# A recurrent layer whose outputs are made with tokens on the partitions, and its two head norms taken along the free axis

## The chip, the cores and the metric

The kernel runs on one core of a Trainium2 chip. The time is device microseconds of one execution, and the number that counts is the median of the runs. A core has TensorE (PE, with its weight loads, PEld), VectorE (DVE), ScalarE (ACT), GpSimd (POOL) and queues that issue transfers (SP's above all). Each engine works off its own instructions in a fixed order; semaphores tie the engines together.

## The reference, cut to what matters

A trunk of two layers over 512 tokens of 1024 features. Layer 0 mixes tokens with a recurrence of 12 heads of 64 (in 6 pairs), beside attention to 256 memory tokens. Layer 1 is chunked attention. Each layer has an output projection and a gated feed-forward part. Here the head norms of the recurrence are what counts:

```python
kk = k_h * per_head(k_k)
kk = kk / jnp.maximum(jnp.sqrt(jnp.sum(kk * kk, axis=-1, keepdims=True)), 1e-12)
k_h = k_h * (1.0 + (a_h - 1.0) * per_head(k_a))
y = wkv7_scan(r_h, w_h, k_h, v_h, -kk, kk * a_h)
mean = jnp.mean(y, axis=-1, keepdims=True)
var = jnp.mean(jnp.square(y - mean), axis=-1, keepdims=True)
y = (y - mean) * lax.rsqrt(var + LN_X_EPS) * per_head(lnx_w) + per_head(lnx_b)
y = y + jnp.sum(r_h * k_h * r_k.astype(f32), axis=-1, keepdims=True) * v_h
out = y.reshape(bsz, seq, D_MIX).astype(h.dtype) * g
```

So there are two sums over the 64 features of each head and token: the key norm (kk) and the group norm (var; the values enter with their mean taken out, so the mean of y is zero).

## The kernel before, in words

Activations lie with features on the 128 partitions and the 512 tokens along the free axis; a tile of 128 features is a pair of heads. The recurrence is solved in 8 chunks of 64 tokens. Three generators work on a pair of heads:

- `prepare` (L566): projections of key, receptance and value (`dense`, L190 on: eight weight tiles in a high and a low part, hence the lines L198, L199 and L203), the decay, the key norm, the products within a chunk (L644), which go through DRAM (d1, Lr) to VectorE. There a forward substitution of 31 steps (L657 to L669, tiles Xs and Xu) runs, and its result goes back through DRAM (d2, Tt).
- `front` (L707): the products of keys and receptances in a chunk (L717, masked on VectorE at L720) and transposes to token rows (L731 to L745).
- `back` (L768): the remaining blocks of the inverse (L776 to L799), the chunk's matrices (L805 to L823), the outputs psy: the part within a chunk (L831) and, in a chain over chunks, the part from the state (L836 makes the next state, L837 adds it on VectorE, L841 adds the state's part to the outputs), then the group norm and the gate.

Both norms use `head_rsqrt` (L546): a tile of squares is the stationary side of four matmuls with a two-column selector (L550), which gives sums with tokens on the partitions, 128x8. VectorE takes the inverse root in ten small instructions (L222 to L226), copies it out to 128x512 (L556), and four transposes (L559) turn it back to features on the partitions. VectorE multiplies by it: L629 for the key norm, L857 for the group norm. After L857 come scale and bias on ScalarE (L858), the bonus on VectorE (L859), and `dst_mix` (L867): the gate (L868), and a transfer to DRAM for the first four pairs, or, for the last two, a split into a high part (L215) and a low part (L216), which the output projection reads.

`weave` (L82) sets the order in which the generators write their instructions: each `yield` states a cost and a wait in ns, and the generator that is furthest behind its share goes next. A scheduler then reorders within its own rules, so that the real order of each engine is seen only in the built program. A round of the loop at L909 runs `back` of pair n-1, `front` of pair n and `prepare` of pair n+1. After the loop, `back` of the last two pairs runs beside the memory attention and the first two tiles of the output projection (`out_ahead`, L317 on), which are started without the last pair's features; `out_proj` adds these, with the residual add at L334, and takes the remaining six tiles. The residual x is loaded (L955) once the recurrent layer's buffers are free.

## Time and profile before

| what | value |
|---|---|
| median of 3 runs | 1376.41 us (1375.87 to 1377.62) |
| profiled execution | span 1375.2 us; the record holds no other time of this execution |
| TensorE's mean granted clock | 0.989 of full speed |
| busy: PE, PEld, VectorE, ScalarE, GpSimd | 1320.1, 1073.8, 827.1, 612.6, 34.0 us |
| chain that ended last | PE 78%, DVE 12%, ACT 4%, DMA 3%, issue 2% |
| transfers | 139.18 MB, mean 101 GB/s |

The span runs from the first to the last instruction. An engine is busy while an instruction of it is in flight; matmuls overlap one another, so a group of matmuls is priced by the distance from its start to the start of what follows it, not by the sum of its durations. Idle time of an engine is given with what ended it. Nearly all of the time after some 385 us is feed-forward and attention, which the change doesn't touch; the recurrent layer lies between some 50 and 372 us.

### The profile page before, as it was taken

To read this page: it belongs to the slowest core of one execution; us is meant where nothing else is said; L and a number is where in the kernel's file an instruction comes from. 1 tells how busy PE (TensorE), PEld (TensorE's weight loads), DVE (VectorE), ACT (ScalarE), POOL (GpSimd) and SP (SyncE) were. 2 spreads that over 40 slices of the span, in tenths; PEclk is the share of its full clock that TensorE was granted. 3 is DMA by queue.
4 is the path that set the end of the run, shared out by engine and by line. 5 is a ranking of instruction groups with operands and counts; after the bars stand their busy time and mean duration, and the time that the engine had idled before them with its cause. 6 is when DMAs were issued, how large, how long until landed. Compare 5 with 4: busy or idle time off the path is not lost.

```text
span 1375.2 us, 20877 instructions
## 1 busy us (share of the span) xinstructions
PE 1320.1 (96%) x8266; PEld 1073.8 (78%) x8266; DVE 827.1 (60%) x1752; ACT 612.6 (45%) x1022; POOL 34.0 (2%) x55
## 2 busy tenths in 40 slices
PE   6989999999799999999999999999999999999996
PEld 4877777777588888888888878786788888888886
DVE  7876788878356655655333667657665565563324
ACT  6556565555234333333222566657443333332321
POOL 3000000000000000000000000000000000000000
PEclk9999999999899999999999999999999999999998
DMA  5366544462132233233232422222223223223332
GB/s 181 112 181 135 107 104 111 104 135 50 52 117 92 92 100 100 92 97 99 84 98 85 157 87 85 82 94 94 92 92 107 92 93 103 96 88 86 106 91 75
DMA packets 63507, 139.18 MB, mean 101 GB/s; under 512 B 24625, under 2 KB 28337, under 8 KB 63409
## 3 DMA queue, kind: packets, MB, share of 16 engines
q1 hardware_dynamic: 60672, 127.89, 29.8%
q0 software_dynamic: 2736, 9.96, 4.2%
q8 instruction: 65, 1.06, 0.3%
q14 instruction: 34, 0.27, 0.1%
HBM read 131.01 MB, written 6.82 MB: 100 GB/s over the span
## 4 chain that ended last, share of the span: by engine, by line
PE 78%; DVE 12%; ACT 4%; DMA 3%; issue 2%; SPq 0%; DVEq 0%; ACTq 0%; POOLq 0%
PE psf L198 12%; PE psf L199 12%; PE psf L203 12%; PE psd L198 10%; PE psd L199 10%; PE psd L203 10%; DVE Xu L667 2%; DVE Xs L669 1%; PE pss L1098 1%; DVE Xs L662 1%; DVE ML L720 1%; DVE wlo L175 1%; PE psd L1048 1%; PE pss L297 1%; ACT whi L169 1%
## 5 line engine op out<-in xcount | busy, mean ns | idle before, releaser
L175 DVE TENSOR_TENSOR wlo<-wraw,whi 128x1024 fp32r<-128x1024 f32 x183 | 219.0, 1197 | 132.3 <-PE psd L203 118.2
L169 ACT CAST whi<-wraw 128x1024 fp32r<-128x1024 f32 (+1 forms) x202 | 207.8, 1030 | 163.9 <-DMA wraw<-in_ffn_out_dram 41.5
L198 PE MATMUL psd<-r1h,whi 128*128 128x512 f32 x336 | 137.6, 410 | 7.5 <-ACT r1h L215 3.8
L198 PE MATMUL psf<-r2h,whi 128*128 128x512 f32 x352 | 137.1, 390 | 0.0
L198 PE MATMUL psf<-r1h,whi 128*128 128x512 f32 x352 | 137.1, 390 | 0.0
L199 PE MATMUL psf<-r1l,whi 128*128 128x512 f32 x352 | 136.9, 389 | 0.0
L199 PE MATMUL psf<-r2l,whi 128*128 128x512 f32 x352 | 136.9, 389 | 0.0
L199 PE MATMUL psd<-r1l,whi 128*128 128x512 f32 x336 | 134.9, 401 | 0.2 <-DVE r1l L216 0.2
L203 PE MATMUL psd<-r1h,wlo 128*128 128x512 f32 x336 | 91.3, 403 | 3.9 <-DMA wlo<-in_wA_dram 3.9
L199 PE MATMUL psd<-f3l,whi 128*128 128x512 f32 (+1 forms) x238 | 88.6, 377 | 0.0
L198 PE MATMUL psd<-f3h,whi 128*128 128x512 f32 (+1 forms) x238 | 88.5, 376 | 0.0
L359 DVE TENSOR_TENSOR tmp<-psf,rho 128x512 f32<-128x512 f32 x44 | 30.4, 692 | 94.7 <-PE psf L203 94.7
L203 PE MATMUL psf<-r1h,wlo 128*128 128x512 f32 x352 | 86.9, 389 | 0.0
L203 PE MATMUL psf<-r2h,wlo 128*128 128x512 f32 x352 | 86.9, 389 | 0.0
L198 PEld LDWEIGHTS psd<-r1h,whi 128*128 128x128 f32 x336 | 65.0, 193 | 23.7 <-ACT r1h L215 4.0
L198 PE MATMUL psd<-r2h,whi 128*128 128x512 f32 (+1 forms) x200 | 77.0, 389 | 0.8 <-ACT r2h L1105 0.7
L199 PE MATMUL psd<-r2l,whi 128*128 128x512 f32 (+1 forms) x200 | 76.4, 385 | 0.7 <-DVE r2l L216 0.7
L198 PEld LDWEIGHTS psf<-r2h,whi 128*128 128x128 f32 x352 | 66.1, 188 | 13.7
L199 PEld LDWEIGHTS psf<-r1l,whi 128*128 128x128 f32 x352 | 66.1, 188 | 13.7
L203 PEld LDWEIGHTS psf<-r1h,wlo 128*128 128x128 f32 x352 | 66.1, 188 | 13.7
L203 PEld LDWEIGHTS psf<-r2h,wlo 128*128 128x128 f32 x352 | 66.1, 188 | 13.7
L199 PEld LDWEIGHTS psf<-r2l,whi 128*128 128x128 f32 x352 | 66.1, 188 | 13.6
(352 smaller groups left out, 2420.9 us busy)
## 6 DMA issues: line engine op xcount, KB each, us to landing
wraw<-in_ffn_in_dram SPq DMA_DIRECT2D x88, 512.0 KB, 3.3
wraw<-in_ffn_out_dram SPq DMA_DIRECT2D x32, 448.0 KB, 3.3
wraw<-in_wA_dram SPq DMA_DIRECT2D x20, 512.0 KB, 3.9
wlo<-in_wA_dram POOLq DMA_DIRECT2D x17, 512.0 KB, 8.0
wraw<-in_w_out_dram SPq DMA_DIRECT2D x16, 512.0 KB, 3.4
wraw<-in_ffn_out_dram SPq DMA_DIRECT2D x16, 512.0 KB, 4.2
wraw<-in_wB_dram SPq DMA_DIRECT2D x8, 512.0 KB, 3.4
Lr<-d SPq DMA_DIRECT2D x24, 128.0 KB, 6.3
```

The costliest lines, as they stand in the source:

```text
L169: SC.copy(hi[:, :n], raw)
L175: V.tensor_tensor(lo[:, :n], raw, hi[:, :n], op=ALU.subtract)
L198: PE.matmul(ps, wh[:, j * P:(j + 1) * P], ah, start=start and n == 0, stop=False)
L199: PE.matmul(ps, wh[:, j * P:(j + 1) * P], al, start=False, stop=False)
L203: PE.matmul(ps, wl[:, j * P:(j + 1) * P], act(k)[0], start=False, stop=stop and n == len(ks) - 1)
L297: PE.matmul(pso[hs, :], vm[l][:, kt, (f * 2 + hh) * 64:(f * 2 + hh + 1) * 64], pts[f, hh, kt], start=kt == 0, stop=kt == 1)
L359: V.tensor_tensor(v[:], pv[:], rho[:], op=ALU.mult)
L662: V.scalar_tensor_tensor(X[:, m, q + 1:], L1[:, :, 0], X[:, m, q:q + 1], X[:, m, q + 1:], op0=ALU.mult, op1=ALU.add)
L667: V.tensor_tensor(uv, L1.rearrange("p i o -> p o i").to_broadcast([P, k, n]), X[:, 0:k, q:q + 1].to_broadcast([P, k, n]), op=ALU.mult)
L669: V.tensor_tensor(X[:, 0:k, q + 1:], X[:, 0:k, q + 1:], uv, op=ALU.add)
L720: V.tensor_tensor(ML[:, h, c4 * 4:c4 * 4 + 4, 0:128], ps[h][:], C("m1").unsqueeze(1).to_broadcast([P, 4, 128]), op=ALU.mult)
L1048: PE.matmul(pt, r1h[:, k, ts], wh[:, ws], start=k == 0, stop=False)
```

## The change

The outputs psy are made the other way round: the operands of L831 and L841 swap sides, so that psy holds tokens of a chunk on the partitions and features along the free axis. The group norm then needs no matmul: VectorE sums the squares along the free axis, takes the inverse root and multiplies. After that, sixteen 64x64 matmuls with the identity turn the result back to features on the partitions, and ScalarE applies scale and bias on its way out of PSUM. In the key norm the squares are turned by four transposes and summed by VectorE from PSUM, in place of the four matmuls with the selector; the way back stays. Some stated costs and waits for `weave` change with it.

```diff
-    def head_rsqrt(sq, sel, fix, bank):
+    def head_rsqrt(sq, bank):
         ps = bank()
         for t in range(4):
-            PE.matmul(ps[:, 2 * t:2 * t + 2], sq[:, t * P:(t + 1) * P], C(sel), start=True, stop=True)
+            PE.transpose(ps[:, t * P:(t + 1) * P], sq[:, t * P:(t + 1) * P], C("ident"))
         a = kt_("hra", (P, 8), bufs=2)
-        fix(a[:], ps[:, 0:8])
+        V.tensor_reduce(a[:], ps[:].rearrange("p (g c) -> p g c", c=64), axis=AX.X, op=ALU.add)
+        V.tensor_scalar(a[:], a[:], 1e-24, None, op0=ALU.max)
         r = rsqrt_small(kp, a[:], 8)
-        yield 700, 3000
+        yield 600, 3500
...
-                PE.matmul(psy[HS[h], c], VT[:, h, c], ML[:, h, c, 64:128], start=c == 0, stop=False)
+                PE.matmul(psy[HS[h], c], ML[:, h, c, 64:128], VT[:, h, c], start=c == 0, stop=False)
...
-                    PE.matmul(psy[HS[h], c], St[HS[h], c], MQ[HS[h], c, 0:64], start=False, stop=c == 7)
+                    PE.matmul(psy[HS[h], c], MQ[HS[h], c, 0:64], St[HS[h], c], start=False, stop=c == 7)
...
         sq = tmp()
         SC.activation(sq[:], yc[:], AF.Square)
-        yield 0, 1700
-        hr = head_rsqrt(sq, "hsm", lambda o, p: V.tensor_scalar(o, p, LN_X_EPS, None, op0=ALU.add), ps_s)
-        yield next(hr)
-        pr_ = next(hr)
+        a = kt_("hra", (P, 8), bufs=2)
+        V.tensor_reduce(a[:], c3(sq[:]), axis=AX.X, op=ALU.add)
+        V.tensor_scalar(a[:], a[:], 1.0 / 64, LN_X_EPS, op0=ALU.mult, op1=ALU.add)
+        r = rsqrt_small(kp, a[:], 8)
+        V.tensor_tensor(c3(yc[:]), c3(yc[:]), r[:].unsqueeze(2).to_broadcast([P, NCH, 64]), op=ALU.mult)
+        yield 0, 5000
         if go is not None:
             yield go
+        pt = ups()
+        for c, h, ap, vp in U:
+            PE.matmul(pt[ap, c], yc[ap, c * 64:c * 64 + 64], cst[ap, I64:I64 + 64], start=True, stop=True)
         pg = ps_l()
         mm3(pg[:], g2h[:], g2l[:], gsh[:], gsl[:], True, True)
-        V.tensor_tensor(yc[:], yc[:], pr_[:], op=ALU.mult)
-        SC.activation(yc[:], yc[:], AF.Identity, scale=Vc("lnx_w", i), bias=Vc("lnx_b", i))
+        yc = tmp()
+        SC.activation(yc[:], pt[:].rearrange("p c t -> p (c t)"), AF.Identity, scale=Vc("lnx_w", i), bias=Vc("lnx_b", i))
         V.tensor_tensor(yc[:], yc[:], bon[:], op=ALU.add)
         dst(i, yc, pg)
-        yield 1080
+        yield 1680
```

The lines below the first edit move down by one, those behind the group norm by six. Three places show how the built order changes. First VectorE, at the key norm of the pair that the third steady round prepares. Xu and Xs are the substitution's tiles, hra the sums, rsq the inverse root. Before:

```order
L667 TENSOR_TENSOR Xu<-Lr,Xs 128x75
L626 TENSOR_SCALAR hra<-pss 128x8
L669 TENSOR_TENSOR Xs<-Xs,Xu 128x5x15
L222 TENSOR_SCALAR rsq<-hra 128x8
L667 TENSOR_TENSOR Xu<-Lr,Xs 128x70
```

And with the change:

```order
L670 TENSOR_TENSOR Xs<-Xs,Xu 128x5x15
L552 TENSOR_REDUCE hra<-pss 128x8
L668 TENSOR_TENSOR Xu<-Lr,Xs 128x70
L553 TENSOR_SCALAR hra<-hra 128x8
L670 TENSOR_TENSOR Xs<-Xs,Xu 128x5x14
L222 TENSOR_SCALAR rsq<-hra 128x8
```

The reduction over 128x512 stands where a small instruction stood, one more small instruction follows it, and the inverse root begins about one substitution step later.

Second VectorE again, at the end of the group norm in the same stretch (bon is the bonus, psl the gate, ML the masked products). Before:

```order
L556 COPY tmp<-rsq 128x512
L857 TENSOR_TENSOR tmp<-tmp,pss 128x512
L859 TENSOR_TENSOR tmp<-tmp,bon 128x512
L720 TENSOR_TENSOR ML<-pss,cst 128x4x128
L868 TENSOR_TENSOR tmp<-tmp,psl 128x512
L720 TENSOR_TENSOR ML<-pss,cst 128x4x128
```

And with the change:

```order
L226 SCALAR_TENSOR_TENSOR rsq<-rsq_2603,rsq 128x8
L854 TENSOR_TENSOR tmp<-tmp,rsq 128x512
L865 TENSOR_TENSOR tmp<-tmp,bon 128x512
L874 TENSOR_TENSOR tmp<-tmp,psl 128x512
L721 TENSOR_TENSOR ML<-pss,cst 128x4x128 x2
```

The copy is gone, the multiply stands ahead of the matmuls that turn the result, and between it and the bonus only PE and ScalarE lie.

Third PE, at the last pair's group norm, among the first two tiles of the output projection (psd). Before, from the second tile's sixth weight tile on:

```order
L199 MATMUL psd<-r1l,whi 128x512
L550 MATMUL pss<-cst,tmp 128x2 x4
L198 MATMUL psd<-r1h,whi 128x512
...
L203 MATMUL psd<-r1h,wlo 128x512 x7
L559 MATMUL pss<-cst,tmp 128x128 x4
L198 MATMUL psd<-r1h,whi 128x512
L199 MATMUL psd<-r1l,whi 128x512
```

And with the change:

```order
L199 MATMUL psd<-r1l,whi 128x512
L860 MATMUL pss<-cst,tmp 64x64 x16
L198 MATMUL psd<-r1h,whi 128x512
...
L203 MATMUL psd<-r1h,wlo 128x512 x7
L198 MATMUL psd<-r1h,whi 128x512 x2
L199 MATMUL psd<-r1l,whi 128x512
```

The sixteen matmuls stand where the sums stood, with the same eight and seven matmuls behind them, and nothing stands where the turned scale stood; the next L198 is the one that needs the last pair.

## Rows read from the trace of the kernel before

**Rows 1.** The page's first part: busy us, share of the span, instructions.

```profile
PE 1320.1 (96%) x8266; PEld 1073.8 (78%) x8266; DVE 827.1 (60%) x1752; ACT 612.6 (45%) x1022; POOL 34.0 (2%) x55
```

**Rows 2.** Busy time by stretch: stretch, length, engines (instructions), PE clock, DMA share, GB/s.

```profile
178.00:220.00 42.00, 40.04 (x509) 31.25 (x509) 34.16 (x121) 23.48 (x43) 3.45 (x4) 1.00 0.56 121
329.00:347.00 18.00, 17.90 (x271) 13.22 (x269) 12.98 (x42) 11.96 (x33) 0.00 (x0) 1.00 0.11 35
375.00:380.00 5.00, 3.14 (x7) 2.48 (x8) 4.24 (x6) 2.38 (x4) 0.00 (x0) 0.50 0.97 344
```

**Rows 3.** PE in order of time, a steady round: start, length, instruction [idle before].

```profile
193.90 1.15 PE L644 MATMUL pss<-KB,AR 64*64 64x64 f32 x32
194.85 0.31 PE L841 MATMUL psl<-MQ,W 64*64 64x64 f32 x4
...
205.71 0.95 PE L550 MATMUL pss<-cst,tmp 128*128 128x2 f32 x8
206.52 0.48 PE L198 MATMUL psd<-r1h,whi 128*128 128x512 f32 x1
...
210.51 0.60 PE L559 MATMUL pss<-cst,tmp 128*128 128x128 f32 x4
211.04 0.69 PE L781 MATMUL pss<-Tl,ML 32*32 32x32 f32 x32
...
231.52 0.63 PE L559 MATMUL pss<-cst,tmp 128*128 128x128 f32 x4 [0.81 <-DVE Xu L667]
```

**Rows 4.** VectorE in order of time: first round (107.80) and steady rounds.

```profile
107.80 0.17 DVE L626 TENSOR_SCALAR hra<-pss 128x8 f32<-128x8 f32 x1 [1.77 <-PE pss L550]
...
189.22 0.23 DVE L667 TENSOR_TENSOR Xu<-Lr,Xs 128x48 f32<-128x48 f32 x1
...
209.36 0.17 DVE L226 SCALAR_TENSOR_TENSOR rsq<-rsq,rsq 128x8 f32<-128x8 f32 x1
209.56 0.43 DVE L556 COPY tmp<-rsq 128x512 f32<-128x512 f32 x1
...
213.40 0.69 DVE L859 TENSOR_TENSOR tmp<-tmp,bon 128x512 f32<-128x512 f32 x1 [1.56 <-ACT tmp L858]
214.00 0.68 DVE L720 TENSOR_TENSOR ML<-pss,cst 128x512 f32<-128x512 f32 x1
...
230.95 0.42 DVE L556 COPY tmp<-rsq 128x512 f32<-128x512 f32 x1
```

**Rows 5.** PE in order of time, the end of the recurrent layer.

```profile
362.48 0.95 PE L550 MATMUL pss<-cst,tmp 128*128 128x2 f32 x8
...
366.84 0.60 PE L559 MATMUL pss<-cst,tmp 128*128 128x128 f32 x4
371.23 0.50 PE L198 MATMUL psd<-r1h,whi 128*128 128x512 f32 x1 [3.79 <-ACT r1h L215]
...
376.86 0.80 PE L198 MATMUL psd<-r1h,whi 128*128 128x512 f32 x1 [2.57 <-DVE xT L334]
...
381.72 0.63 PE L199 MATMUL psd<-r1l,whi 128*128 128x512 f32 x1
382.15 0.52 PE L198 MATMUL psd<-r1h,whi 128*128 128x512 f32 x1
```

**Rows 6.** ScalarE in order of time, the same stretch.

```profile
355.38 0.63 ACT L848 ACTIVATE tmp<-tmp 128x512 f32<-128x512 f32 x1
368.26 0.81 ACT L858 ACTIVATE tmp<-tmp,vec 128x512 f32<-128x512 f32 x1 [12.26 <-DVE tmp L857]
...
372.62 1.04 ACT L169 CAST whi<-wraw 128x1024 fp32r<-128x1024 f32 x1 [1.45 <-PE psd L199]
```

**Rows 7.** VectorE in order of time, the same stretch.

```profile
371.21 0.69 DVE L216 TENSOR_TENSOR r1l<-tmp,r1h 128x512 fp32r<-128x512 f32 x1 [0.69 <-ACT r1h L215]
```

**Rows 8.** The reduction of the memory attention (L270): ns min/median/max, first and last start.

```profile
L270 DVE TENSOR_REDUCE mst<-pss x16: 670/684/692, 320.3 to 867.4; 128x2 f32<-128x512 f32 x16
```

**Rows 9.** SP's queue in order of time, the same stretch: the loads of x.

```profile
371.96 1.75 SPq L955 DMA_DIRECT2D xT<-in_xT_dram  x4
```

More of the change, by code (lines that the diff above doesn't have):

```diff
@@ L625, in keys @@
             SC.activation(sq[:], kn[:], AF.Square)
-            hr = head_rsqrt(sq, "hs1", lambda o, p: V.tensor_scalar(o, p, 1e-24, None, op0=ALU.max), ps_s)
+            hr = head_rsqrt(sq, ps_s)
             yield next(hr)
@@ L848, in back @@
         SC.activation(sq[:], yc[:], AF.Square)
-        yield 0, 1700
-        hr = head_rsqrt(sq, "hsm", lambda o, p: V.tensor_scalar(o, p, LN_X_EPS, None, op0=ALU.add), ps_s)
-        yield next(hr)
-        pr_ = next(hr)
+        a = kt_("hra", (P, 8), bufs=2)
[4 more added lines that the diff above has]
+        yield 0, 5000
         if go is not None:
             yield go
+        pt = ups()
+        for c, h, ap, vp in U:
+            PE.matmul(pt[ap, c], yc[ap, c * 64:c * 64 + 64], cst[ap, I64:I64 + 64], start=True, stop=True)
         pg = ps_l()
         mm3(pg[:], g2h[:], g2l[:], gsh[:], gsl[:], True, True)
-        V.tensor_tensor(yc[:], yc[:], pr_[:], op=ALU.mult)
-        SC.activation(yc[:], yc[:], AF.Identity, scale=Vc("lnx_w", i), bias=Vc("lnx_b", i))
+        yc = tmp()
+        SC.activation(yc[:], pt[:].rearrange("p c t -> p (c t)"), AF.Identity, scale=Vc("lnx_w", i), bias=Vc("lnx_b", i))
         V.tensor_tensor(yc[:], yc[:], bon[:], op=ALU.add)
         dst(i, yc, pg)
-        yield 1080
-    BACK_COST = 2 * 650 + 2 * MC + 4 * 1100 + 1700 + 6 * 150 + 7 * 150 + 700 + 1080
+        yield 1680
+    BACK_COST = 2 * 650 + 2 * MC + 4 * 1100 + 1700 + 6 * 150 + 7 * 150 + 1680
     mixd = dp.tile([4, P, S], F32, name="mixd", tag="mixd")
```

## The prediction

> **What bounds the kernel now.** I read the busy line first: PE has matmuls in flight for 96% of the span [rows 1], so a gain must take work from PE or close a gap in front of it. The recurrent layer holds nearly all that the change touches, so I then read busy times by stretch. Its steady part is a round of some 42 us, four of them from 136 to 304 us; in one, PE is busy for 40 us of 42 and VectorE for 34 [rows 2]. The gaps are small, and the question is which engine ends each part of a round.
>
> PE in order of time answers that [rows 3]. A round has two fixed points: the matmuls that turn the group norm's scale (L559, 210.51 us) and those that turn the key norm's scale (L559 again, 231.52 us). Ahead of the first PE did not wait. So the half of the round that ends there, half B, is set by PE. Ahead of the second PE idled 0.81 us for VectorE. So half A, between the two, is set by VectorE, which from the bias add at 213.40 to the copy that ends at 231.37 runs without a gap worth naming [rows 4]: it works off the 31 steps of the forward substitution, and the key norm's small instructions stand between them.
>
> Then the end of the recurrent layer. The last pair's group norm has nothing recurrent behind it. Its sums stand on PE at 362.48, behind output-projection matmuls, and its turned scale at 366.84; PE then waits 3.79 us for the finished pair and 2.57 us more for a bank [rows 5]. This is the longest hole in the layer, and the chain through it is: multiply, ScalarE's scale and bias, bias add, gate, cast, split [rows 6, 7].
>
> **The change part by part.**
>
> *Key norm (six times).* Four matmuls with a two-column moving side become four transposes. The first take 0.81 us until the next matmul starts (205.71 to 206.52), the second 0.53 (210.51 to 211.04) [rows 3]: PE saves 0.28 us. VectorE adds a sum over 128x512. Such a reduction costs 684 ns here [rows 8]; queued behind other work it takes about 0.60 of the engine, the distance of a 0.69 us instruction from its successor (213.40 to 214.00) [rows 4]. The clamp stays at 0.16. In half A this addition is on the path, since VectorE ends that half.
>
> The Trainium skill speaks against it ("VectorE: DVE Perf Modes", Rules for kernel authors): a reduction on a hot path is called the slowest operation of the engine, better restructured away. By the row it is as slow as a bias add of the same shape (0.69) and no slower. By the page the outcome would be the first rival, 1381.1; by the row it is the sum below.
>
> *Group norm (six times).* On PE the sums (0.81) and the turned scale (0.53) go; sixteen 64x64 matmuls come. The nearest row is the sixteen of L644, 193.90 to 194.85, 0.95 us [rows 3]: 0.39 saved. On VectorE a copy (0.42) and a multiply (0.69, as the bias add of the same shape) become a reduction and a multiply: +0.26. The path to the bias add shortens. Before, 2.89 us lie between L559's start and the bias add (210.51 to 213.40), of them 1.56 of waiting [rows 3, 4]. After, the turned result goes straight through ScalarE: 0.95 on PE, 0.81 on ScalarE [rows 6] and two hand-overs, 2.0 us. VectorE starts its long run 0.9 us earlier against PE.
>
> *Outputs with swapped operands.* Both sides have 64 columns before and after, in the same number of passes: 0. Bounds: one weight load of a state less or more per chunk, hidden under output projections or weights in the rounds; I keep +-0.2.
>
> *A round, half A.* -0.9 for the earlier bias add, +0.60 for the reduction. In two of three rounds the new order also puts one more pair of substitution steps ahead of the copy, 0.23 us each, 0.5 with the gaps [rows 4]. Sum +0.2, and -0.3 without that pair. PE's saving there is not seen: PE would only wait longer.
>
> *Half B.* The sums' 0.81 leave PE. In the new order about 0.5 us more of the projection stands in this half, taken from half A where PE waits anyway. The new chain (copy and square on ScalarE, 0.6 each; reduction and multiply, 0.69 each; eleven small instructions 0.20 apart [rows 4, 6]) takes 4.8 us and some 0.5 of hand-overs after the last output matmul. The order holds 22 to 24 wide matmuls over it, 5.2 to 5.7 us at the 0.24 that they take at the end of the layer, so it is covered; where that cover is thin, a gap of up to 0.5 us opens. Sum -0.3, with -0.8 if nothing moved. A round: about -0.2; four rounds -0.9. Bounds: -0.7 a round if PE's saving counted in full (-2.8), +1.0 a round if the reduction, the pair of steps and a wait for the key product all count against only the earlier bias add (+4.0).
>
> *First round and first pair.* Here VectorE waited 1.77 us for the key norm's sums [rows 4], so the reduction lies bare in the chain: +0.6, less 0.28 on PE; with the wait behind it I take +0.5 (0 to +0.8).
>
> *The pair before last.* It runs beside memory attention, where PE is busy 17.9 of 18 us [rows 2]: PE's saving counts, -0.4 (0 to -0.5).
>
> *The last pair.* In the new order the sixteen matmuls take the place of L550, and nothing takes the place of L559. Their input is ready by about 359.8: the square ends at 356.0 [rows 6], then reduction, eleven small ones and multiply, 3.6 us. So no wait at 362.48. They end at 363.43. The fifteen projection matmuls behind them took 3.55 us (0.81 after 362.48, to 366.84; 0.24 each), so PE is at the waiting matmul at 366.98. From ScalarE's scale and bias (368.26) to PE's restart (371.23) it was 2.97 us; now that chain starts at 363.5, so the operand is there at 366.5 and the wait of 3.79 goes [rows 5, 6]. The split of the low half ended at 371.90 and will end at 367.15, and the loads of x that are issued on its end (371.96) go out 4.75 earlier [rows 7, 9]. What is late next: the weights of the third output tile. ScalarE's cast waits for PE to release a buffer (372.62); a second cast, two subtractions and the residual add follow on it, and PE gets its bank at 376.86 [rows 5, 6]. These links keep their lengths, from 367.4 on: bank at 371.95. Gain 4.9 us. PE will then idle longer there, 3.6 us instead of 2.57.
>
> The clock is the unknown. After the 3.79 us gap the granted clock fell to 0.50 from 375 to 380 us, its lower level of 1.2 GHz [rows 2], and matmuls stayed 0.43 us apart (381.72 to 382.15) until then [rows 5]. Between 376.86 and 382.15 this costs 5.3/2 = 2.65 us. I assume the same length of slow running behind the remaining gap. Bounds: none (2.65 more gained), or as long as from the first restart, 10.9 us (2.8 us given back): -2.1 to -7.5.
>
> **The sum.** -0.9 + 0.5 - 0.4 - 4.9 = -5.7 us on the profiled execution's span of 1375.2; that gives 1369.5. The median of the runs, 1376.41, is 1.2 above this span, so I forecast 1370.7.
>
> **The rivals.**
>
> *VectorE becomes the bound (slower).* Place: the key norm in the five rounds that hold a substitution. If reduction (0.60), pair of steps (0.5) and a wait of about 1 us for the key product behind it all add up, and half B ends on VectorE too, a round gets 2.0 us longer: +10, less 5.3 at the end, +4.7: 1381.1. For it: VectorE's unbroken run in half A. Against: the bias add comes earlier, and VectorE has some 8 us of idle time per round. It decides from a round that is 1.1 us longer than now. 8 in 100. This is what the caution of the Trainium skill above ("VectorE: DVE Perf Modes", Rules for kernel authors) comes to in this kernel; the trace bears it out in half A only.
>
> *The end gives little.* If the gap that is left keeps the clock low for as long as before, the end brings 2.1, and the rounds come out even: 1376.4 - 2.1 + 0.5 = 1374.8. For it: the remaining gap is nearly as long as the one that went. 21 in 100.
>
> *PE's saving counts everywhere.* Five rounds at -0.7, the end 4.9, the pair before last 0.4: -8.8, 1367.6. Against it speaks the wait in half A. 11 in 100.
>
> *Forecast* as above, 60 in 100, its own range 1367 to 1374.
>
> **Numbers.** The range 1366.0 to 1377.0 takes in the end at both bounds and the rounds from -2.8 to about +3. A measurement here can tell about 0.2%, 2.75 us, so faster means below 1373.7. There lie 0.56 of the forecast's 0.60 and all of the third rival: 0.67. Same: the second rival and 0.03 of the forecast, 0.24. Slower, above 1379.2: the first rival and the last 0.01, 0.09.
>
> **What would show it.** The wait of 3.79 us before the first output tile gone, the wait for the bank (2.57) grown by about a microsecond, and the loads of x issued some 4.8 us earlier against the last output matmul. In the rounds: waits of PE at the key norm's turn grown from 0.8 towards 1.5 us, waits of VectorE for L550 and L559 gone from the group norm, rounds of 41.5 to 42.5 us. I am wrong if rounds exceed 43 us, if PE waits at the new sixteen matmuls, or if the low clock after the end outlasts some 8 us.

## The result, and the profile after

The changed kernel takes 1384.77 us (median of 13 runs, 1379.51 to 1392.24) against 1376.89 (13 runs, 1374.77 to 1382.22) for the kernel before: ratio 1.0051, with a 95% interval of [1.0035, 1.0067]. It is **slower by 7 us**, half a percent: little, but clear of the noise. The forecast was 1370.7 with a range to 1377.0, so sign and size were both missed.

The page's first part of the changed kernel, and its line by core:

```profile
PE 1328.6 (96%) x8362; PEld 1077.7 (78%) x8362; DVE 834.2 (60%) x1758; ACT 614.5 (44%) x1022; POOL 33.7 (2%) x55
```

```profile
core 0: 1390.5 us, clock 0.977
```

PE has 96 more instructions and is busy 8.5 us longer [rows 1]. By the counts in the rows the group norm now issues 32 of them for a pair where it issued 12, and the key norm four fewer, for six pairs. They are short ones; what changed is the speed. Span times mean granted clock, an estimate of what the span would be at full clock, is 1375.2 x 0.989 = 1360.1 before and 1390.5 x 0.977 = 1358.5 after. Taken from each run's device time and clock, the median of this product is 1361.8 for the changed kernel (13 runs) and 1360.8 for the kernel before (the 29 runs of experiment 2). **By this estimate the two kernels would take the same time at full clock, to about 1 us; the difference in time is the size of the clock that TensorE lost.** That is a balance: the changed kernel does less work at the end and waits more before it, and the waits are what the low clock follows.

This execution was the slowest of the 13; a second profile comes from another one (1385.73 us, span 1384.0, clock 0.984). By fixed points of PE:

| stretch, end in the kernel before | forecast | first profile | second profile |
|---|---|---|---|
| start to the third pair's key turn (146.66) | +0.5 | +3.4 | +4.0 |
| to the group turn of the fourth round (295.28) | -0.9 | +9.1 | +6.2 |
| to the last pair's turn or sums (362.48) | -0.4 | +7.1 | +4.0 |
| to the end | -4.9 | -4.3 | -5.4 |
| sum | -5.7 | +15.3 | +8.8 |

I call *lost clock* the sum of (1 - granted clock) x 5 us over slices of 5 us from 0 to 400 us. It is 10.2 us before, 27.2 in the first and 18.8 in the second profile: in the second the 8.6 us more are nearly the whole 8.8 us of the span. By stretch it is not all clock: in the rounds (second line of the table) some 5 of the 9.1 us and 3.4 of the 6.2 are lost clock, and the rest is mostly the new waits themselves.

**The end went as forecast.** PE in order of time, changed kernel (start, length, instruction, idle before):

```profile
373.86 0.48 PE L842 MATMUL psd<-AR,Lr 64*64 64x64 f32 x4 [0.27 <-DVE AR L838]
...
382.04 1.15 PE L860 MATMUL pss<-cst,tmp 64*64 64x64 f32 x32
...
391.64 0.79 PE L198 MATMUL psd<-r1h,whi 128*128 128x512 f32 x1 [3.43 <-DVE xT L334]
```

and SP's queue:

```profile
386.92 1.78 SPq L961 DMA_DIRECT2D xT<-in_xT_dram  x4
```

The wait of 3.79 us is gone, and the bank wait grew from 2.57 to 3.43 [rows 5]. From the last output matmul to the loads of x it is 13.1 us (386.92 - 373.86) where it was 17.6 (371.96 [rows 9] - 354.38): 4.5 earlier, 4.8 forecast.

**The rounds did not.** In two profiles of this kernel three rounds from key turn to key turn took 42.6, 47.4, 45.2 and 42.9, 42.8, 46.3 us, where before they took 42.1 to 42.8. PE now waits at the sixteen matmuls (L860). PE, then VectorE, in the second round:

```profile
192.62 0.63 PE L560 MATMUL pss<-cst,tmp 128*128 128x128 f32 x4 [1.47 <-DVE Xu L668]
...
216.42 1.63 PE L860 MATMUL pss<-cst,tmp 64*64 64x64 f32 x32 [2.01 <-DVE tmp L854]
```

```profile
210.51 0.69 DVE L851 TENSOR_REDUCE hra<-tmp 128x8 f32<-128x512 f32 x1 [0.24 <-ACT tmp L849]
212.59 0.43 DVE L777 STREAM_TRANSPOSE Tl<-Tt 32x256 f32<-32x256 f32 x1 [1.39 <-DMA Tt<-d]
212.96 0.12 DVE L852 TENSOR_SCALAR hra<-hra 128x8 f32<-128x8 f32 x1
...
215.59 0.69 DVE L854 TENSOR_TENSOR tmp<-tmp,rsq 128x512 f32<-128x512 f32 x1
```

VectorE works in order. Between the reduction (L851) and the small instruction behind it (L852) stands L777, the transpose of the solved blocks, and it waits 1.39 us for their load from DRAM (Tt). All of the norm's root and the multiply (L854) stand behind, and PE behind them. The place is not new. In the kernel before, both transposes (L776 there) stood among the root's small instructions as well:

```profile
206.78 0.42 DVE L776 STREAM_TRANSPOSE Tl<-Tt 32x256 f32<-32x256 f32 x1
207.69 0.43 DVE L776 STREAM_TRANSPOSE Tl<-Tt 32x256 f32<-32x256 f32 x1
```

They waited in none of the four rounds; what is new is that the load is late for them. Busy time by stretch, changed kernel, columns as in [rows 2]:

```profile
212.00:217.00 5.00, 2.99 (x29) 2.29 (x28) 3.28 (x14) 2.11 (x2) 0.86 (x1) 0.99 0.42 89
217.00:222.00 5.00, 5.00 (x70) 4.41 (x68) 2.29 (x4) 1.51 (x3) 0.00 (x0) 0.50 0.82 167
```

Behind the wait of 2.01 us the clock is at its lower level (0.50, 1.2 GHz): the wait costs 2 us, the slow matmuls behind it 2.5 more from 217 to 222 us. Not every such wait is followed by that. In the second profile PE waits as long in the fourth round, and the clock stays full:

```profile
305.43 1.15 PE L860 MATMUL pss<-cst,tmp 64*64 64x64 f32 x32 [2.00 <-DVE tmp L854]
```

```profile
305.00:310.00 5.00, 4.57 (x122) 4.31 (x124) 3.42 (x7) 2.09 (x4) 0.45 (x1) 1.00 0.66 129
```

Why the load is late shows in the queues, third round, SP and GpSimd, changed kernel:

```profile
253.51 0.36 SPq L180 DMA_DIRECT2D wraw<-in_wA_dram  x1
254.08 3.08 SPq L676 DMA_DIRECT2D Tt<-d  x4
```

```profile
253.78 0.86 POOL L173 DMA_DIRECT2D wlo<-in_wA_dram  x1 [9.03 <-ACT wlo L172]
```

The weights of the next pair (wraw, 512 KB, and the accumulating load of their low half, wlo, 512 KB) go out ahead of the solved blocks, and L777 waited for these until 263.04, 2.21 us. Before, the blocks went out at 244.76 and wlo only at 245.81. In the second round it is wlo alone: 206.34 against 206.97 for the blocks, where before the blocks went out at 202.18 and wlo at 203.68. In the fourth the blocks still go out first, at 298.61, but wlo follows at 298.92 where it came 0.98 us behind them, and L777 waits 1.66 us. Where the wait falls differs too: in the second and fourth rounds it stands inside the norm's chain (L860 waits 2.01 and 1.74 us); in the third the wait of 2.21 us stands behind the multiply, L860 waits 0.54 us, and the matmuls that take the blocks (L782) wait 1.24.

**Memory attention lost as much.** PE beside the memory attention, changed kernel:

```profile
334.95 0.33 PE L837 MATMUL psl<-W,MQ 64*64 64x64 f32 x4 [1.62 <-DVE W L838]
...
336.26 0.44 PE L837 MATMUL psl<-W,MQ 64*64 64x64 f32 x4 [0.46 <-DVE W L838]
```

```profile
330.00:335.00 5.00, 3.38 (x23) 2.34 (x21) 5.00 (x11) 1.89 (x6) 0.00 (x0) 1.00 0.17 26
335.00:350.00 15.00, 14.27 (x74) 8.57 (x75) 9.44 (x30) 8.02 (x26) 0.00 (x0) 0.54 0.19 49
```

PE waits 1.62 us for the second state update of the pair before last, and then runs 15 us at a mean clock of 0.54, 6.9 us lost. Before, PE waited 0.38 us there and ran memory attention at 1.00 [rows 2]. VectorE was busy for all of 330 to 335 with work that stands ahead of the update:

```profile
331.58 1.28 DVE L216 TENSOR_TENSOR r1l<-tmp,r1h 128x512 fp32r<-128x512 f32 x2
332.78 0.69 DVE L270 TENSOR_REDUCE mst<-pss 128x2 f32<-128x512 f32 x1
333.38 1.22 DVE L175 TENSOR_TENSOR wlo<-wraw,whi 128x1024 fp32r<-128x1024 f32 x1
...
334.63 0.27 DVE L838 SCALAR_TENSOR_TENSOR W<-psl,dE,VT 128x64 f32<-128x64 f32 x1
```

The subtractions L216 stood ahead of this update in the kernel before too, from 316.82 us; L175 (1.22 us) did not, there it starts at 327.38, behind the fifth update.

### The profile page after: what moved, and what is told of

It is laid out like the page before. It is cut to its first block, busy times and chain, and to the rows that moved or that the text cites. A ratio compares the mean times of both kernels' runs of the same rounds, so it can differ in the third digit from the quotient of the medians.

```text
span 1390.5 us, 21086 instructions
## 1 busy us (share of the span) xinstructions
PE 1328.6 (96%) x8362; PEld 1077.7 (78%) x8362; DVE 834.2 (60%) x1758; ACT 614.5 (44%) x1022; POOL 33.7 (2%) x55
## 3 DMA queue, kind: packets, MB, share of 16 engines
q8 instruction: 66, 1.08, 0.3%
## 4 chain that ended last, share of the span: by engine, by line
PE 78%; DVE 12%; ACT 4%; DMA 4%; issue 2%; SPq 0%; DVEq 0%; ACTq 0%; POOLq 0%
PE psf L198 11%; PE psf L199 11%; PE psf L203 11%; PE psd L198 10%; PE psd L199 10%; PE psd L203 10%; DVE Xu L668 2%; DMA Tt<-d 1%; DVE Xs L670 1%; PE pss L1104 1%; PE pss L718 1%; PE pss L297 1%; PE psd L1054 1%; PE pss L287 1%; DVE wlo L175 1%
## 5 line engine op out<-in xcount | busy, mean ns | idle before, releaser
L175 DVE TENSOR_TENSOR wlo<-wraw,whi 128x1024 fp32r<-128x1024 f32 x183 | 219.0, 1197 | 133.0 <-PE psd L203 117.6
L198 PE MATMUL psd<-r1h,whi 128*128 128x512 f32 x336 | 138.2, 412 | 4.6 <-DVE xT L334 3.4
L198 PE MATMUL psf<-r2h,whi 128*128 128x512 f32 x352 | 137.1, 390 | 0.0
L198 PE MATMUL psf<-r1h,whi 128*128 128x512 f32 x352 | 137.1, 390 | 0.0
L198 PE MATMUL psd<-f3h,whi 128*128 128x512 f32 (+1 forms) x238 | 88.5, 376 | 0.0
L198 PEld LDWEIGHTS psd<-r1h,whi 128*128 128x128 f32 x336 | 65.7, 196 | 20.3 <-DVE xT L334 3.9
L198 PE MATMUL psd<-r2h,whi 128*128 128x512 f32 (+1 forms) x200 | 77.0, 389 | 0.8 <-ACT r2h L1111 0.7
L198 PEld LDWEIGHTS psf<-r2h,whi 128*128 128x128 f32 x352 | 66.1, 188 | 13.7
L198 PEld LDWEIGHTS psf<-r1h,whi 128*128 128x128 f32 x352 | 66.1, 188 | 13.7
```

Source lines behind the costliest of these rows:

```text
L175: V.tensor_tensor(lo[:, :n], raw, hi[:, :n], op=ALU.subtract)
L198: PE.matmul(ps, wh[:, j * P:(j + 1) * P], ah, start=start and n == 0, stop=False)
```

## The experiments

The theory after the first profile: the solved blocks' load falls behind the next pair's weights, VectorE stands still for it with the group norm queued behind, PE waits, and the clock falls. The rivals: A, VectorE's added work itself (reductions, a longer half A) is the cost; B, memory attention loses apart from the rounds; C, the profiled execution was a chance run. Ratios are to the kernel before on the same chip, whose median there is 1376.8 to 1379.4 us, so experiments are compared by ratio. The intervals of the ratios are some 2 to 4 us to either side, so a difference of 4 us between two of them is known to about 3. Each edit also moves some other instructions in the built order.

**1. The changed kernel again** (no edit).

> The changed kernel itself, for a second profile. By T the waits of VectorE for the solved blocks' load and of PE at the turn-back stand in the same rounds again (over 1 us in at least two of four), whatever the total (1379.5 to 1392 so far). A rival (C) says that the profile first shown was a chance run whose low clock in the memory attention made the difference: then the clock is 0.985 or more here, the time below 1382, and rounds of 42 us.

1385.73 us, the second column of the table. L777 waits 1.08, 1.76 and 1.93 us in the first, third and fourth rounds, L860 0.57, 0.96 and 2.00, the second state update 1.98, and memory attention has the low clock again (0.56 over 330 to 345). Waits over 1 us come back in three rounds at L777, at L860 in one only, where two were expected. The pattern stands in the main; rival C falls.

**2. Each part alone.**

```diff
 key_only: the kernel before, and in prepare
-            hr = head_rsqrt(sq, "hs1", ...)
+            hr = key_rsqrt(sq, ps_s)     (the changed head_rsqrt)
 group_only: the changed kernel with the old key norm
-            hr = head_rsqrt(sq, ps_s)
+            hr = head_rsqrt(sq, "hs1", ...)
```

> The kernel before with the key norm's part of the change alone (transposes, VectorE's sum, its stated cost and wait); outputs and group norm as before. Three theories. (T) In the changed kernel VectorE stands still for the solved blocks' load (the transposes of L777 wait for it, up to 2.2 us), the group norm's small steps are queued behind, the turn-back matmuls (L860) wait up to 2.0 us and the clock falls behind that. (K) The sum over 128x512 on VectorE lengthens every round by itself. (G) The group norm's new chain is too long for the projection matmuls that stand over it. By T this kernel comes to 1376.9 plus 0 to 4, since the load is some 0.6 us later but no turn-back waits for VectorE's small steps; by K to 1385 or more (all of the loss, +8, plus the end's gain that is missing here, +4); by G to within 1 of 1376.9.

> The changed kernel with the key norm of before (two-column matmuls, clamp on VectorE, its stated cost and wait). By T the load of the solved blocks comes some 0.6 us earlier, the wait behind it shrinks but does not go: 1374 to 1380. By K all of the loss in the rounds goes and the end's gain of 4.3 us stays: 1372.6. By G the loss stays: 1384 or more.

Key part alone: 1382.49, 1.0045 [1.002, 1.007]. Group part alone: 1378.17, 1.0002 [0.9987, 1.0017]. The first lies in none of its three ranges, between T's and K's; the second lies in T's. The key part alone costs nearly as much as the whole. But its product of time and clock has a median of 1360.8 over the runs, as the kernel before: by that estimate it adds no time at full clock, so VectorE's added work is not a cost as such (rival A). Whether it costs through longer waits and the clock behind them is left for experiments 4, 6 and 10. The group part's product is 1356.6, 4.2 us under the kernel before: in its profile the end is 4.5 us shorter, and lost clock takes that back. Its profile shows where, in a wait and a stretch:

```profile
320.94 0.33 PE L836 MATMUL psl<-W,MQ 64*64 64x64 f32 x4 [1.35 <-DVE W L837]
```

```profile
320.00:340.00 20.00, 18.30 (x84) 10.60 (x85) 11.50 (x35) 8.93 (x30) 0.00 (x0) 0.57 0.18 43
```

0.43 x 20 = 8.6 us lost in memory attention. In the kernel before this wait is 0.38 us. In the changed kernel as a whole the product is 1361.8: by the same estimate the two parts together lose some 5 us at full clock that neither loses alone.

**3. The solved blocks' transposes behind the norm.** A copy of one column makes the transposes of L777 stand behind the multiply in VectorE's order.

```diff
         V.tensor_tensor(c3(yc[:]), c3(yc[:]), r[:]..., op=ALU.mult)
+        if go is None:
+            V.tensor_copy(Tl[:, 0, 0:1], yc[:, 0:1])
```

> The changed kernel with one 128x1 copy on VectorE behind the group norm's multiply that keeps the transposes of the solved blocks (L777) behind that multiply on VectorE in all rounds; nothing else. By T the waits at the turn-back (2.0 and 1.7 us in rounds 2 and 4) fall to under 0.6 and the low clock behind them goes: 1376 to 1380. By K and by G nothing changes: 1384 to 1386.

1381.03, 1.0019 [1.0002, 1.0036]: 1.0051 - 1.0019 = 0.0032, 4.4 us back, and 1 us above T's range. The rounds keep full clock, and L860 (here L862) waits 0.33 us. The late load itself is still there, now in front of other matmuls:

```profile
213.36 1.15 PE L862 MATMUL pss<-cst,tmp 64*64 64x64 f32 x32 [0.33 <-DVE tmp L854]
...
259.24 0.69 PE L782 MATMUL pss<-Tl,ML 32*32 32x32 f32 x30 [2.14 <-DVE Tl L777]
```

Memory attention still loses 8.6 us of clock, although PE waits only 0.63 us at the second state update (here L175 stands behind it):

```profile
325.51 0.33 PE L837 MATMUL psl<-W,MQ 64*64 64x64 f32 x4 [0.63 <-DVE W L838]
```

```profile
325.00:345.00 20.00, 18.82 (x85) 10.79 (x85) 11.39 (x35) 8.94 (x30) 0.00 (x0) 0.57 0.18 43
```

So the theory holds for the rounds, and rival B stands beside it.

**4. Filling the gap at the key turn** (key part alone).

```diff
+        for _ in range(5):
+            PE.matmul(pt[:], blk1[:], zw[:], start=True, stop=True)
         for t in range(4):
             PE.transpose(pt[:, t * P:(t + 1) * P], bc[:, ...], C("ident"))
```

> The kernel with the key norm's part alone, and five more 128x512 matmuls (0.22 us each at full clock, overwritten afterwards) on PE directly ahead of the key norm's turn, where PE waits 1.25 to 1.82 us for VectorE; nothing else, and VectorE's work is the same. Theory W1, the clock: the key norm costs its 5.7 us (1382.5 against 1376.8) because the wait that grew from 0.8 to 1.5 us lets the clock fall in most runs. Then 5 x 0.22 = 1.1 us of work in the wait costs next to nothing and the time falls to 1376 to 1379, with a narrower spread than 1374 to 1394. Theory W2, VectorE: the reduction and what queues behind it make the rounds longer as such; then the time stays at 1382 to 1384, or rises by the 1 us in the first pair, where the wait lies elsewhere.

1394.12, 1.0129 [1.0109, 1.0149]: a miss. The turn's wait fell to 0.3 us, but the built order changed, with new waits of PE of up to 3.40 us, the longest behind a transpose (L795) that itself waits 3.62 us for the solved blocks. It says nothing of the question.

**5. A shorter VectorE queue in memory attention, by the third output tile** (group part alone). VectorE's subtraction for the third output tile's weights (L175, 1.22 us) is replaced by the way through ScalarE and an accumulating load.

```diff
+                lo_on[0] = 1 if pre and m == 2 else 0
                 w = load_w(A["w_out"][l, m])
+                lo_on[0] = 0
```

> The kernel with the group norm's part alone (1378.2), and the low half of the third output tile's weights made as those of the two ahead of it are (ScalarE and an accumulating DMA) in place of the subtraction on VectorE (L175, 1.2 us), which stands in memory attention between the first two state updates, where PE then waits 1.35 us (L836) and the clock is 0.50 to 0.70 from 320 to 340 us. Theory M: this wait starts the low clock, which costs about 4.6 us and hides the end's gain: 1373 to 1375, full clock from 320 to 340. Rival: the stretch loses its clock through many small waits, whatever stands there: 1377 to 1379.

> As the last, and the 128x1 copy that keeps the transposes of the solved blocks behind the group norm's multiply on VectorE. If the load that VectorE waits for costs through the turn-back, 1 to 2 us below the last kernel (1372 to 1374); if the wait only moves to the matmuls that need the transposed blocks (1.68 us at L781 in one round of the kernel with the group norm's part alone), the same within 1 us.

> The kernel before with the same edit of the third output tile's weights, as a control. There the subtraction stands behind the fifth state update and the clock is full from 304 to 355 us, so theory M expects no change: 1376 to 1378. If it gains 3 us or more, what the last two kernels gain is not the clock in memory attention but the subtraction itself, or the cast and subtraction at the end.

1378.68, 1.0013 [0.9989, 1.0038]; with the edit of experiment 3 besides, 1383.12, 1.0033 [1.0004, 1.0062]; the same edit in the kernel before, 1378.48, 1.0007 [0.9991, 1.0023]. The first two miss what theory M expected; the third, the control, hardly changes, as expected. The wait stays at 1.31 us, and this edit could not shorten it. In the kernel with the group part alone L175 stands behind VectorE's second update, not ahead of it as in the changed kernel:

```profile
320.61 0.27 DVE L837 SCALAR_TENSOR_TENSOR W<-psl,dE,VT 128x64 f32<-128x64 f32 x1
...
321.40 1.21 DVE L175 TENSOR_TENSOR wlo<-wraw,whi 128x1024 fp32r<-128x1024 f32 x1
```

What stood ahead of the update there are four subtractions of r1l (L216).

**6. Without the accumulating load.** The low half's load is cut to eight columns, in all three kernels.

```diff
-            SC.activation(lo[:, :n], raw, AF.Copy, scale=-1.0)
-            GP.dma_start(lo[:, :n], src, accum_op=ALU.add)
+            SC.activation(lo[:, :n], raw, AF.Copy, scale=-1.0 / 1024)
+            GP.dma_start(lo[:, :8], src[:, 0:8], accum_op=ALU.add)
```

> The changed kernel with the accumulating load of the weights' low half (L173, 512 KB each, 19 times in the recurrent layer) cut to 8 of 1024 columns; the low half that it completes is left out, so the products lose their low part. Theory D: with the change the solved blocks' load (Tt) goes out just behind this load and the weights' own (254.08 us behind 253.51 and 253.78 in round 3; before, 244.76 ahead of 245.81), lands late, and VectorE, then PE wait. Then the waits at L777 (2.21, 1.93, 1.66 us) shrink to under 0.7, those at L860 to under 0.7, and the difference to the kernel before with the same cut falls from 8 us to 0 to 3. Rival: the rounds are longer because VectorE has more to do (the reduction); then the difference stays at 6 to 9.

> The kernel before with the same cut, the measure for the last one: the low half of the weights in the recurrent layer is left out here too. It loses the wait of 3.9 us for the first such load (L203 at 97.66 us) and little else: 1370 to 1376.

> The kernel with the key norm's part alone, with the accumulating load of the weights' low half cut to 8 of 1024 columns as in the two kernels before (the low half is left out). With the full load this part costs 5.7 us (1382.5 against 1376.8). If that comes through the late load of the solved blocks (D), it comes within 2 us of the kernel before with the same cut (1372.0). If it comes through the longer waits at the key norm's turn (W1) or VectorE's work, 1376 to 1378.

Changed kernel 0.998 [0.997, 0.999], kernel before 0.9958 [0.9945, 0.9971], key part alone 0.9984 [0.9967, 1.0001]. With the load gone, the change costs 0.0022 or 3.0 us instead of 7.0: about 4 us hang on that load, which agrees with experiment 3. L777 no longer waits, the rounds keep full clock, and L860 waits little:

```profile
251.00 1.15 PE L860 MATMUL pss<-cst,tmp 64*64 64x64 f32 x32 [0.29 <-DVE tmp L854]
...
319.93 0.33 PE L837 MATMUL psl<-W,MQ 64*64 64x64 f32 x4 [1.96 <-DVE W L838]
```

The wait in memory attention is as long as in the changed kernel, and 6.9 us of clock are lost there. The key part alone still costs 0.0026, 3.6 us, where it cost 6.2 with the load: a part of its cost at least is not the late load, and how much is, the intervals leave open.

**7. The four subtractions on GpSimd** (group part alone, with the edit of 5).

```diff
-            split_to(r1h[:, m], r1l[:, m], t_[:])
+            SC.copy(r1h[:, m], t_[:])
+            GP.tensor_tensor(r1l[:, m], t_[:], r1h[:, m], op=ALU.subtract)
```

> The kernel with the group norm's part alone, with VectorE relieved in memory attention: the four low-half subtractions of the mixed values that come back (r1l, L216, 0.6 us each) go to GpSimd, and the low half of the third output tile's weights is made by ScalarE and an accumulating load. Before the second state update VectorE then has about 2.4 us less to do, where PE waited 1.35 us. Theory M: PE finds the state ready, the clock stays full from 320 to 340 us (it was 0.50 to 0.70), and the end's gain shows: 1372 to 1375. Rival: the clock falls there all the same, or another wait takes its place: 1377 to 1380.

1379.67, 1.0014 [1.0000, 1.0029]: no gain, as the rival had it. The wait fell only to 1.02 us; GpSimd's work held VectorE up by some 2 us ahead of it. GpSimd, then VectorE:

```profile
315.76 2.51 POOL L897 TENSOR_TENSOR r1l<-tmp,r1h 128x512 fp32r<-128x512 f32 x2 [18.82 <-ACT r1h L896]
```

```profile
315.36 0.22 DVE L669 TENSOR_TENSOR Xu<-Lr,Xs 128x35 f32<-128x35 f32 x1
315.85 1.23 DVE L669 TENSOR_TENSOR Xu<-Lr,Xs 128x28 f32<-128x28 f32 x1
317.12 1.19 DVE L671 TENSOR_TENSOR Xs<-Xs,Xu 128x28 f32<-128x28 f32 x1
318.34 0.18 DVE L669 TENSOR_TENSOR Xu<-Lr,Xs 128x24 f32<-128x24 f32 x1
```

**8. The weights held back** (changed kernel). The next pair's first weights wait until the solved blocks have landed.

```diff
+        if behind is not None:
+            GP.tensor_copy(raw[0:64, 0:1], behind[0:64, 7, 0:1])
```

> The changed kernel with one added condition: the load of the next pair's first projection weights waits until the solved blocks of the pair two before it have landed (GpSimd writes 64 of their values into the weights' tile first). So these blocks no longer stand behind a 512 KB load. By theory D the waits of VectorE at L777 and of PE at L860 and at the matmuls that take the blocks fall under 0.8 us in all rounds and 3 to 5 us are won: 1380 to 1382. Rival: the weights now come late instead, PE waits for them (L198 or L203 on the weights' load), and nothing is won: 1384 to 1390.

1392.52, 1.0102 [1.0081, 1.0123]: the rival, and worse than its range. The weights are now late (PE waits 3.49 us for wlo at L205, and 4.45 at L862 in the first round); the rounds lose 12.0 us of clock. One thing it shows besides: with the order of the work so shifted, memory attention loses none. In both orders that were tried, the load that goes second keeps an engine waiting.

**9. The subtractions later** (both kernels, with the edit of 5). `flush_mix` no longer runs ahead of memory attention but between its steps; three of its four subtractions come behind the state updates.

```diff
-           (told(chain(q_mem(...), flush_mix(), mA), "mem"),
+           (told(chain(q_mem(...), mixed(mA, flush_mix(), (8, 9, 10, 11))), "mem"),
```

> The changed kernel with VectorE relieved in memory attention without GpSimd: three of the four low-half subtractions of the mixed values are issued later, behind the state updates, and the low half of the third output tile's weights is made by ScalarE and an accumulating load. By theory M PE's wait for the second state update (1.62 and 1.98 us in two profiles) falls to under 0.5 us, the clock stays full there and 4 to 7 us are won: 1378 to 1381. Rival: the clock falls all the same through the chain of short matmuls that follows: 1383 to 1386.

> The same edit in the kernel with the group norm's part alone (1378.2): by theory M the end's gain shows, 1372 to 1375, below the kernel before; by its rival 1377 to 1380.

Changed kernel: 1381.45, 1.0016 [0.9995, 1.0037], 0.0035 or 4.8 us back. Its profile has no wait at the second state update and full clock from 310 to 345 us, but 3.4 us of clock go from 345 to 355, behind a wait of 1.84 us, and as much from 300 to 310, behind one of 2.52 us at L860 (here L862). Group part alone: 1377.53, 0.9991 [0.9974, 1.0007], in the rival's range. There the wait shrank from 1.35 to 0.24 us and the clock stays up where it was 0.57:

```profile
320.88 0.33 PE L838 MATMUL psl<-W,MQ 64*64 64x64 f32 x4 [0.24 <-DVE W L839]
...
329.33 0.70 PE L287 MATMUL pss<-cst,Ei 128*128 128x128 f32 x4 [1.53 <-DVE Ei L279]
...
339.91 0.50 PE L184 MATMUL psl<-gsh,Xs 128*128 128x512 f32 x1 [1.84 <-ACT Xs L215]
```

```profile
320.00:340.00 20.00, 16.39 (x163) 10.29 (x162) 14.65 (x51) 13.71 (x45) 0.02 (x1) 1.00 0.45 110
```

Lost clock there falls from 8.5 to 1.7 us, but there are two new waits of 1.53 and 1.84. The first is the stop of the rounds once more: VectorE waits for solved blocks ahead of the L279 that PE needs.

```profile
328.61 0.43 DVE L778 STREAM_TRANSPOSE AR<-Tt 32x256 f32<-32x256 f32 x1 [2.37 <-DMA Tt<-d]
```

The second comes from ScalarE, where the postponed casts stand. The kernel ends even with the kernel before. It is the best version found that holds a part of the change, and not measurably faster.

**10. Where the key part loses its clock.** Key part alone again, twice, and key part for the last four pairs only.

```diff
-            hr = key_rsqrt(sq, ps_s)
+            hr = head_rsqrt(sq, "hs1", ...) if i < 2 else key_rsqrt(sq, ps_s)
```

> The kernel with the key norm's part alone once more, for a second profile: the first profiled execution (1374.2) was the fastest of twelve, with a clock of 0.990 and waits of 1.5 us at the key norm's turn that cost nothing. Theory D: where it is slow (over 1380) the clock falls behind a late load of the solved blocks (VectorE waiting over 1 us at their transposes, PE over 1 us at the matmuls that need them, L798). Rival W1: it falls behind the waits of 1.5 us at the key norm's turn (L576), with the load in time.

> The kernel with the key norm's part, but with the key norm of before for the first two pairs, where VectorE's chain lies bare and PE waits 1.82 us at the second pair's turn, in a stretch (92 to 136 us) whose clock is already low behind the first weights. Theory W1a: the 5.7 us that the key norm's part costs in most runs are lost there (clock 0.88 to 0.92 in five of ten profiles of kernels with this part, 0.96 in all eight without it): 1377 to 1379. Theory W1b: they are lost behind the four waits of 1.5 us in the rounds, which stay: 1381 to 1384.

> A third profile of the kernel with the key norm's part alone, in the hope of one of its slow runs (8 of 12 took over 1380 us; the two profiled ones took 1374.2 and 1377.0). If it is slow: by W1a the lost clock lies between 92 and 136 us, by W1b behind the key norm's turns from 147 to 280 us (granted clock under 1.00 within 10 us of L576), by D behind a late load of the solved blocks (VectorE waiting over 1 us at L793).

Key part for the last four pairs only: 1380.36, 1.0020 [1.0005, 1.0036], between the two ranges, so some 3 of the key part's 6 us may hang on the first two pairs; the intervals overlap. The two further executions of the key part alone came out at 1376.97 and 1382.10. Their waits at the key turn are alike (1.82, 1.59, 1.54, 1.5, 1.3 us) with full clock from 136 to 305 us in both; their lost clock is 10.2 and 15.3. The 5.1 us between the two times are clock alone, all of it between 335 and 350 us, in memory attention. That is none of the three places that were expected. First key_again, then key_look, both by stretch:

```profile
335.00:350.00 15.00, 14.86 (x273) 12.29 (x272) 10.04 (x31) 9.88 (x27) 0.00 (x0) 1.00 0.01 4
```

```profile
335.00:350.00 15.00, 15.00 (x183) 12.30 (x184) 8.30 (x28) 8.36 (x23) 0.00 (x0) 0.66 0.01 3
```

The nearest wait is 0.44 us in one and 0.47 in the other. So the same program, with the same waits, does or doesn't lose the clock there. What tips it stays open.

## Why the prediction was wrong

**Half B, "so it is covered": wrong.** This step failed first. I counted the matmuls over the norm's chain against the chain's own length and never asked what else stands in VectorE's queue between its links. The transposes of the solved blocks stood there, before and after, and they wait on a transfer. Before, it came in time. After, it goes out behind the low half of the next weights in two rounds, behind both loads in one and closer ahead of them in the fourth, and VectorE, which must go from L851 to L854 without a stop, stops; the queues were read for the loads of x alone. The forecast for the rounds was -0.9; they cost 9.1 and 6.2. Where no transpose waited in the chain, the count was about right: L860 waited 0 to 0.57 us, and a gap of up to 0.5 was allowed for. Where one did, PE waited 0.54 to 2.01 us. Experiments 3 and 6 show about 4 us of the 7 to hang on this.

One reading under this step was wrong as well. "Ahead of the first PE did not wait" holds for the round shown, at 210.51 us; at the same place in the other three steady rounds PE waited 0.29 to 0.31 us for VectorE, so half B ended on VectorE already. One of them, kernel before:

```profile
252.43 0.66 PE L559 MATMUL pss<-cst,tmp 128*128 128x128 f32 x4 [0.29 <-DVE tmp L556]
```

**The pair before last, -0.4: wrong.** That PE was busy 17.9 of 18 us [rows 2] said that PE's saving would count. What the runs show in its place is that PE gets to the second state update earlier than VectorE: a wait of 0.38 us became 1.62 and 1.98, and memory attention lost 6.9 us of clock in both profiles. This wait was not in the working, nor were the VectorE subtractions ahead. The size of the loss does not follow the wait: in the eight profiles of all kernels where it is 0.63 to 1.98 us, 5 to 9 us of clock are lost, 8.6 behind the shortest; in the other twelve the clock holds through the state updates, but in some it falls later in the same stretch (5.1 us in the slower execution of experiment 10). So the wait is where the low clock mostly starts; that it is the cause isn't shown. Experiment 9, which takes it away, gives 4.8 us back.

**First round, +0.5: too small.** The reduction lay bare as expected: the key turn's wait of PE is now 1.83 us behind VectorE, where 1.09 behind ScalarE stood before. What came behind it was a spell of low clock that I had not priced. First the changed kernel, then the kernel before:

```profile
110.00:115.00 5.00, 3.17 (x90) 2.77 (x90) 2.96 (x13) 3.82 (x6) 0.86 (x1) 0.95 0.93 154
115.00:120.00 5.00, 5.00 (x18) 3.73 (x18) 4.88 (x9) 0.73 (x1) 0.00 (x0) 0.71 0.72 187
```

```profile
110.00:115.00 5.00, 4.28 (x20) 3.32 (x20) 2.83 (x6) 2.73 (x4) 0.86 (x1) 1.00 0.25 41
115.00:120.00 5.00, 3.88 (x44) 3.34 (x45) 4.46 (x8) 3.31 (x7) 0.00 (x0) 1.00 0.92 189
```

From 90 to 136 us the changed kernel loses 5.1 us of clock in both its profiles, the kernel before 1.7. Of the 3.4 more, 1.7 lie here, behind the key turn; the other 1.7 lie from 95 to 105, behind a wait for the first weights that is 4.36 and 4.44 us where it was 3.90. The profiles with the key part lose 1.7 to 5.1 us from 90 to 136; those without it 1.7, every one.

**"The clock is the unknown": right, but priced in one place only.** I bounded it behind the gap at the end, where nothing changed for the worse. It decided much of the rest. The Trainium skill ("TensorE: Matmul & The Clock Gate", A second HAM failure mode: psum-queue depth-cycling) tells of a kernel in which short idle spells of PE between groups of matmuls came often enough for the clock to swing between its two levels. By that a wait of a microsecond or two can cost more than its length, and the rows agree in part: 2.01 us of waiting, then 0.50 from 217 to 222. No row says when it does: the second profile kept 1.00 behind a wait of 2.00 us, and the key part alone kept it behind waits of 1.5 us in every round.

**Right:** the end (-4.3 and -5.4 for -4.9; the 3.79 wait gone, the bank wait up by 0.9 for about a microsecond); the reduction's price; the key turn's waits from 0.8 to about 1.5; no more work on the path in half A at full clock, by the estimate of experiment 2. On the price, the changed kernel's lines in groups (idle before, and what ended it, behind the bar):

```profile
L854 DVE TENSOR_TENSOR tmp<-tmp,rsq 128x512 f32<-128x512 f32 x6 | 4.1, 691 | 0.2
L552 DVE TENSOR_REDUCE hra<-pss 128x8 f32<-128x512 f32 x6 | 4.1, 686 | 2.4 <-PE pss L550 2.4
L851 DVE TENSOR_REDUCE hra<-tmp 128x8 f32<-128x512 f32 x6 | 4.1, 681 | 3.3 <-ACT tmp L849 3.3
```

686 and 681 ns against 684 in [rows 8], and no more than a multiply of that shape (691): the first rival's reason, a VectorE that is bound by reductions, isn't what made the kernel slower. Its other half, that half B ends on VectorE, came true through the late load. No rival held that mechanism, so that the measured time lies nearest to this rival is luck. Rounds beyond 43 us and a wait at the sixteen matmuls were named as what would prove me wrong, and both came.

**Account of the 7 us.** Late load and stopped norm in the rounds, about 4 (experiments 3 and 6); memory attention, about 5 (experiment 9); the key part's spells of low clock, some 6 alone (experiment 2) and partly the same microseconds; less the 4.5 gained at the end. The parts overlap, each is known to some 3 us, and what sets off the key part's spells isn't shown. Nor is why leaving the key part out (experiment 2) takes away the whole loss.

## What to carry to other kernels

Where work goes from PE's chain to VectorE's, read VectorE's built order between the first and the last link and ask of each instruction in between what it waits for, transfers above all; an in-order engine adds every such wait to the chain. Price a new PE wait of 1 to 2 us not by its length alone but also with the lower clock that can follow it (here 2.5 us or none behind 2.0, 6.9 behind 1.6), and take span times granted clock of several runs to see whether a change costs work or clock. A gain shown at one place (4.5 us at the end) says nothing of the sum while the kernel's clock elsewhere hangs on gaps of a microsecond.

## What was not expected of the hardware

- One program's times spread with its clock: key part alone, 1374.18 to 1394.48 us over 12 runs, with two executions 5.1 us apart on the same waits.
- The length of PE's wait does not tell how much clock goes: 2.00 us was followed by full clock (second profile of the changed kernel), 0.63 us by 8.6 us of lost clock (experiment 3).
- A VectorE instruction of 0.2 us took 1.23 and 1.19 while GpSimd's two subtractions ran (experiment 7). The Trainium skill ("SBUF — State Buffer", SBUF: two separate sides) tells of a port pair that a VectorE operation with two SBUF inputs and a GpSimd operation that reads SBUF hold in turn, each for its whole instruction. The trace agrees: the operands of the two VectorE instructions, Lr, Xs and Xu, lie there, and the next one takes 0.18 us once GpSimd is done.
